# Feed-forward features transposed by DVE in 32x32 blocks and placed by DMAs through DRAM, with gate and up chunks issued ahead of the down parts

## The chip, the cores and the metric

The kernel runs on one core of one Trainium2 chip. What is measured is the device time of one execution, in microseconds (us), lower is better. The engines are named as in the profile: PE (TensorE matmul), PEld (its weight load), DVE (VectorE), ACT (ScalarE), POOL (GpSimd) and SP (SyncE, which here only issues DMAs; "SPq" is its queue).

## The reference

A stack of four transformer layers and then one hybrid block, for 256 tokens of width 1024, all in float32. The mixers of the four layers are differential attention, stick-breaking attention, sliding-window attention with sinks, and differential attention again. The part that the change touches is the feed-forward block that ends each of the four layers:

```python
D_MODEL = 1024; SEQ = 256; DEPTH = 4
FFN_HIDDEN = -(-8 * D_MODEL // (3 * 256)) * 256        # 2816

def swiglu(h, w_gate, w_up, w_down):
    return (jax.nn.silu(h @ w_gate) * (h @ w_up)) @ w_down

for i in range(DEPTH):
    hn = rms_norm(x, norm_gains[i, 0])
    ...                                                # m = the mixer of layer i
    x = x + rms_norm(m, norm_gains[i, 1])
    f = swiglu(rms_norm(x, norm_gains[i, 2]), ffn_w_gate[i], ffn_w_up[i], ffn_w_down[i])
    x = x + rms_norm(f, norm_gains[i, 3])
```

## The kernel before

**Tiles.** The 256 tokens are two blocks b = 0 and 1 of 128 tokens. All big products keep float32 accuracy by splitting each operand into a high part that the matmul takes exactly (`hi`) and the rest (`lo`), and adding three matmuls: hi x hi, hi x lo, lo x hi. The stationary operand is the transposed activations (features on the 128 partitions, tokens along the row): `hnT` for the normalised input of a layer, `hT` for the hidden features of the feed-forward block, `oT` for the output of a mixer. The moving operand is a 128x512 piece of a weight matrix. A `gemm` over a contraction of 1024 is thus 8 x 3 = 24 matmuls into one PSUM tile `acc`.

**Weights.** All weights are streamed. A chunk is 512 columns of a weight matrix. SP loads it in `raw` tiles (three buffers of 1 MB); for each half of a `raw` tile ACT writes `hi` and DVE writes `lo` into a `w` tile (11 buffers, four of them to a chunk). A `w` tile is free again when both blocks have used it.

**Steps.** The work is a list of steps, one for each chunk, and block 1 runs one step behind block 0: (step 1, b 0), (step 0, b 1), (step 2, b 0), and so on. In the feed-forward block a gate step makes silu(gate) into `sg`, an up step multiplies it in (`scalar_tensor_tensor` on DVE), and the product, 128 tokens x 512 features, must become four 128x128 columns of `hT`. Before, `xpose_split` does this: four PE transposes into the PSUM tile `tr`, then `hi` by ACT and `lo` by DVE into `hT`. The 2816 hidden features are five groups of 512 (gate and up as chunks of their own) and a last group of 256 (`gate_up`, one chunk with both). They are contracted in three parts of 8, 8 and 6 columns (groups 0 and 1, groups 2 and 3, groups 4 and 5), each with two down chunks (j = 0, 1) whose sums are collected in `facc`. The tile `hT` has one buffer for each block, so the `hT` of a part can only be written when the part before has been used up.

**Order of the instructions.** Nothing is issued in the order of the code. Each operation is recorded, with its dependencies, the order in which buffers of a ring are reused, and an estimated cost; `schedule` then tries many list schedules with randomly drawn priorities (`seed`), keeps the one whose estimate is shortest, and `issue` writes it out as a fixed order for each engine. Every engine works through its own list strictly in order, and waits at an instruction whose inputs are not ready. All instructions are issued from one line of the file, so the profile's rows all read L522 and are told apart by the names of the tiles.

Of the kernel before, what the change touches and what calls it, by code (L numbers as in the profile page):

```python
# [10 lines left out]
F32 = mybir.dt.float32  # L11
# [3 lines left out]
AF = mybir.ActivationFunctionType  # L15
ALU = mybir.AluOpType
# [4 lines left out]
P = 128  # L21
D = 1024
KT = D // P
# [93 lines left out]
class _Program:  # L117
# [14 lines left out]
    DRAIN = 110.0  # L132
    SPARE = 3000.0
    window = 6
    tries, local, seed = 60, 120, 3
    pace = 1.1
    stick, stick_back = 3000.0, 1e9

# [390 lines left out]
class _Net:  # L529
# [711 lines left out]
    def ffn_steps(self, li):  # L1241
        nc, a = self.nc, self.a
        wg, wu, wd = a["ffn_w_gate"][li], a["ffn_w_up"][li], a["ffn_w_down"][li]
        st = {}

        def begin(b):
            if b == 0:
                st["g_post"] = self.load_gain(a["norm_gains"][li, 3])
                st["facc"] = self.S8("facc").rearrange("p (b n) -> p b n", b=NB)
            st["hnT", b], st["r", b] = self.prenorm(b, 2 * li + 1)  # L1250

        def gate_up(ch, part, kt):
            def fn(b):
                ps = self.gemm(b, st["hnT", b], ch)
                s, n = self.t2g(b, "sg"), ch.n // 2
                nc.scalar.activation(s[:, :n], ps[:, :n], AF.Silu, scale=st["r", b])
                nc.vector.scalar_tensor_tensor(s[:, :n], ps[:, n:], st["r", b], s[:, :n], op0=ALU.mult, op1=ALU.mult)
                self.xpose_split(b, s, st["hT", part, b], kt, n=n // P)
            return fn

        def gate(ch, first):
            def fn(b):
                if first:
                    begin(b)
                ps = self.gemm(b, st["hnT", b], ch)
                s = self.t2g(b, "sg")
                nc.scalar.activation(s[:, :ch.n], ps[:, :ch.n], AF.Silu, scale=st["r", b])
                st["sg", b] = s
            return fn

        def up(ch, part, kt):
            def fn(b):
                ps = self.gemm(b, st["hnT", b], ch)
                s = st["sg", b]
                nc.vector.scalar_tensor_tensor(s[:, :ch.n], ps[:, :ch.n], st["r", b], s[:, :ch.n], op0=ALU.mult,
                                               op1=ALU.mult)
                if kt == 0:
                    st["hT", part, b] = self.TB(b, "hT")
                self.xpose_split(b, s, st["hT", part, b], kt, n=ch.n // P)
            return fn  # L1280

        def down(ch, part, j):
            def fn(b):
                ps = self.gemm(b, st["hT", part, b], ch)
                f = st["facc"][:, b, j * 512:(j + 1) * 512]
                if part == 0:
                    nc.scalar.activation(f, ps, AF.Copy)
                else:
                    nc.vector.tensor_tensor(f, ps, f, op=ALU.add)
                if part == 2 and j == 1:  # L1290
                    self.postnorm(b, [st["facc"][:, b, 0:512], st["facc"][:, b, 512:1024]], st["g_post"])
            return fn

        base = 0
        for part, nkt in enumerate((8, 8, 6)):
            kt = 0
            while kt < nkt:
                m = min(4, nkt - kt)
                c0 = (base + kt) * P
                if m == 2:  # L1300
                    ch = self.chunk_of([(wg, c0, m * P), (wu, c0, m * P)], 0, KT)
                    self.step(ch, gate_up(ch, part, kt))
                else:
                    ch = self.chunk(wg, 0, KT, c0, m * P)
                    self.step(ch, gate(ch, part == 0 and kt == 0))
                    ch = self.chunk(wu, 0, KT, c0, m * P)
                    self.step(ch, up(ch, part, kt))
                kt += m
            for j in range(2):
                ch = self.chunk(wd, base, nkt, j * 512, 512)  # L1310
                self.step(ch, down(ch, part, j))
            base += nkt

    def ssm_prep_tasks(self):
        nc, a = self.nc, self.a
# [551 lines left out]
```

## Time and profile before

| | |
|---|---|
| median of 3 runs | 1373.03 us (1371.23 to 1373.67) |
| the profiled execution | 1374.15 us, of which the span of its instructions is 1372.3 us |
| PE busy | 1356.4 us of the span, 99% |
| DVE, ACT, POOL busy | 910.8, 769.2 and 204.9 us |
| granted TensorE clock, mean | 0.996 of full speed |
| moved by DMA | 244.72 MB, mean 178 GB/s |

The profile is of one execution. Matmuls overlap, and the busy time of a short group of matmuls contains the time in which its last one still drains; what a group costs is better read from the chain of work, which gives the distance from one group to the next. Idle time of an engine that is not the bottleneck costs nothing.

### The profile page before, as it was taken

What the parts mean: (1) busy time and instruction counts of PE and PEld (TensorE: products, weight loads), DVE (VectorE), ACT (ScalarE), POOL (GpSimd) and SP (SyncE); (2) the same over time, 40 slices, a digit from 0 to 9 for tenths busy, and PEclk for the clock granted to TensorE, in tenths of its full rate; (3) what the DMA queues carried; (4) which work ended last, traced back from release to release, by engine and by line L of the source; (5) the groups of instructions that cost most, each with busy time, mean ns of one, the idle gap of its engine ahead of it and who ended that gap; (6) DMA issues with size and microseconds to landing.
All of it is one profiled execution on the core that took longest, in us unless ns stands there. A gap on an engine that the chain in (4) does not pass through costs nothing.

```text
span 1372.3 us, 17953 instructions
## 1 busy us (share of the span) xinstructions
PE 1356.4 (99%) x6825; PEld 1119.8 (82%) x6825; DVE 910.8 (66%) x1339; ACT 769.2 (56%) x1269; POOL 204.9 (15%) x331
## 2 busy tenths in 40 slices
PE   9999999999999999999999999999999999999998
PEld 6788888888878888888778888888888888887886
DVE  7977756558665655559967545598866455686493
ACT  6667554437876544447665434465665444564582
POOL 1010067433000069202001000010000000020000
PEclk9999999999999999999999999999999999999999
DMA  8553665455442666645425555554536555476550
GB/s 305 190 185 103 238 229 190 153 204 193 153 154 92 221 220 219 196 156 167 159 87 200 184 186 182 188 170 153 184 107 245 186 184 169 148 239 189 184 192 31
DMA packets 134341, 244.72 MB, mean 178 GB/s; under 512 B 5248, under 2 KB 27008, under 8 KB 134256
## 3 DMA queue, kind: packets, MB, share of 16 engines
q1 hardware_dynamic: 134256, 243.59, 52.8%
q8 instruction: 53, 0.87, 0.3%
q14 instruction: 32, 0.26, 0.1%
HBM read 236.90 MB, written 6.67 MB: 177 GB/s over the span
## 4 chain that ended last, share of the span: by engine, by line
PE 89%; DVE 6%; DMA 2%; ACT 1%; issue 1%; POOL 0%; SPq 0%; ACTq 0%; DVEq 0%
PE acc L522 77%; PE tr L522 3%; DVE w L522 2%; PE z L522 1%; PE sS L522 1%; PE sc L522 1%; DVE rp L522 1%; DMA raw<-in_a_w_in_dram 1%; PE o L522 1%; DVE q L522 1%; PE Y L522 1%; PE asT L522 1%; PE oB L522 0%; PE oC L522 0%; DMA raw<-in_w_ple_gate_dram 0%
## 5 line engine op out<-in xcount | busy, mean ns | idle before, releaser
L522 PE MATMUL acc<-w,hnT 128*128 128x512 f32 (+1 forms) x3552 | 842.8, 391 | 2.1 <-ACT w L522 1.3
L522 PEld LDWEIGHTS acc<-w,hnT 128*128 128x128 f32 x3552 | 651.9, 189 | 135.3 <-ACT w L522 2.1
L522 DVE TENSOR_TENSOR w<-raw,w 128x1024 fp32r<-128x1024 f32 (+1 forms) x431 | 518.6, 1219 | 180.6 <-ACT w L522 170.5
L522 ACT ACTIVATE w<-raw 128x1024 fp32r<-128x1024 f32 (+1 forms) x431 | 442.0, 1041 | 184.4 <-PE acc L522 149.4
L522 PE MATMUL acc<-w,hT 128*128 128x512 f32 x1056 | 252.8, 392 | 0.4 <-DVE hT L522 0.4
L522 PEld LDWEIGHTS acc<-w,hT 128*128 128x128 f32 x1056 | 196.0, 188 | 40.4 <-DVE hT L522 0.8
L522 PE MATMUL acc<-w,oT 128*128 128x512 f32 x480 | 119.9, 397 | 0.0
L522 PEld LDWEIGHTS acc<-w,oT 128*128 128x128 f32 x480 | 88.7, 188 | 18.1 <-issue 0.3
L522 POOL TENSOR_TENSOR po_r<-po_v,neghalf 128x1 f32<-128x1 f32 x16 | 11.9, 746 | 478.4 <-DVE po_v L522 478.4
L522 ACT ACTIVATE sg<-acc,pn_r 128x512 f32<-128x512 f32 (+1 forms) x48 | 31.0, 649 | 86.8 <-PE acc L522 86.8
L522 DVE SCALAR_TENSOR_TENSOR sg<-acc,pn_r,sg 128x512 f32<-128x512 f32 (+1 forms) x48 | 33.8, 705 | 58.9 <-PE acc L522 35.0
L522 POOL TENSOR_TENSOR pg<-pg 128x128 f32<-128x128 f32 x96 | 61.6, 669 | 38.5 <-DMA pg<-scrP 36.0
L522 ACT ACTIVATE hT<-tr 128x512 fp32r<-128x512 f32 (+1 forms) x48 | 26.6, 556 | 53.3 <-PE tr L522 53.2
L522 DVE TENSOR_TENSOR hT<-tr,hT 128x512 fp32r<-128x512 f32 (+1 forms) x48 | 30.7, 642 | 27.0 <-ACT hT L522 27.0
L522 POOL TENSOR_TENSOR pn_r<-pn_v,neghalf 128x1 f32<-128x1 f32 x20 | 17.6, 882 | 189.9 <-DVE pn_v L522 175.1
L522 DVE TENSOR_TENSOR facc<-acc,facc 128x512 f32<-128x512 f32 x32 | 21.9, 686 | 33.0 <-PE acc L522 32.9
L522 ACT ACTIVATE hnT<-gx 128x512 fp32r<-128x512 f32 x36 | 22.7, 630 | 26.5 <-DVE gx L522 26.4
L522 POOL TENSOR_TENSOR pt<-pp 128x256 f32<-128x256 f32 x32 | 28.9, 914 | 42.3 <-PE ke L522 41.6
L522 ACT ACTIVATE ad_e<-sc,ad_nm 128x128 f32<-128x128 f32 (+1 forms) x64 | 26.1, 421 | 12.9 <-DVE ad_nm L522 12.5
L522 ACT ACTIVATE sqj<-x 128x512 f32<-128x512 f32 x40 | 24.9, 623 | 11.3 <-DVE x L522 10.8
L522 POOL TENSOR_TENSOR ad_r<-ad_v,neghalf 128x4 f32<-128x4 f32 x8 | 9.5, 1182 | 135.4 <-DVE ad_v L522 135.4
L522 DVE TENSOR_TENSOR hnT<-gx,hnT 128x512 fp32r<-128x512 f32 x36 | 25.3, 704 | 4.8 <-ACT hnT L522 4.2
(232 smaller groups left out, 1119.4 us busy)
## 6 DMA issues: line engine op xcount, KB each, us to landing
raw<-in_ffn_w_gate_dram SPq DMA_DIRECT2D x40, 1024.0 KB, 5.2
raw<-in_ffn_w_up_dram SPq DMA_DIRECT2D x40, 1024.0 KB, 5.1
raw<-in_ffn_w_down_dram SPq DMA_DIRECT2D x32, 1024.0 KB, 5.2
raw<-in_a_w_in_dram SPq DMA_DIRECT2D x22, 1024.0 KB, 5.2
raw<-in_ffn_w_down_dram SPq DMA_DIRECT2D x16, 768.0 KB, 4.6
raw<-in_b_w_in_dram SPq DMA_DIRECT2D x12, 1024.0 KB, 5.2
raw<-in_w_in_dram SPq DMA_DIRECT2D x12, 1024.0 KB, 5.2
raw<-in_a_w_out_dram SPq DMA_DIRECT2D x8, 1024.0 KB, 5.0
```

The costliest lines, as they stand in the source:

```text
L522: r = getattr(getattr(self.nc, op.eng), op.call)(*op.args, **op.kw)
```

## The change

For the five groups of 512 features, the up step no longer transposes on PE. DVE transposes the product in 32x32 blocks (one instruction, `transpose`, into a tile `hx`), four DMAs of 64 KB put the rows of 32 partitions each in their place in a scratch tensor in DRAM (`scrH`), and one DMA of 256 KB loads it back as `hl`, now with features on the partitions. ACT writes `hi` and DVE `lo` of `hT` from `hl`. `hx` and `hl` come from the ring `t2a`, three tiles of 128x512 for each block. The last group of 256 still goes through PE.

The steps get another order. Before: groups 0, 1, down part 0, groups 2, 3, down part 1, groups 4, 5, down part 2. After: groups 0, 1, 2, down part 0, groups 3, 4, down part 1, group 5, down part 2. So a part's down steps follow the gate and up of one more group. The features of groups 2 and 4 have no place in `hT` until the down steps of the part before are done, so their `load` is recorded behind these. The seed of the schedule search changes from 3 to 6, and as the search runs over the whole program, the order of the instructions changes everywhere.

```diff
@@ -132,7 +132,7 @@
-    tries, local, seed = 60, 120, 3
+    tries, local, seed = 60, 120, 6
@@ -1268,16 +1268,35 @@
-        def up(ch, part, kt):
+        def up(ch, g, now):
             def fn(b):
                 ps = self.gemm(b, st["hnT", b], ch)
                 s = st["sg", b]
                 nc.vector.scalar_tensor_tensor(s[:, :ch.n], ps[:, :ch.n], st["r", b], s[:, :ch.n], op0=ALU.mult,
                                                op1=ALU.mult)
-                if kt == 0:
-                    st["hT", part, b] = self.TB(b, "hT")
-                self.xpose_split(b, s, st["hT", part, b], kt, n=ch.n // P)
+                t = self.t2a(b, "hx")
+                nc.vector.transpose(t.rearrange("p (q c t) -> p c q t", q=4, c=4),
+                                    s.rearrange("p (c q h) -> p c q h", c=4, q=4))
+                d = self.dp.tile([4, P, P], F32, name=f"scrH{li}_{g}_{b}")
+                for i in range(4):
+                    nc.sync.dma_start(out=d[i].rearrange("(q h) x -> h q x", q=4),
+                                      in_=t[32 * i:32 * i + 32].rearrange("h (q x) -> h q x", q=4))
+                st["d", g, b] = d
+                if now:
+                    load(g, b)
             return fn
+
+        def load(g, b):
+
+            part, kt = g // 2, 4 * (g % 2)
+            if kt == 0:
+                st["hT", part, b] = self.TB(b, "hT")
+            t = self.t2a(b, "hl")
+            nc.sync.dma_start(out=t.rearrange("p (i x) -> p i x", i=4), in_=st["d", g, b].rearrange("i p x -> p i x"))
+            v = t.rearrange("p (i c t) -> p c i t", i=4, c=4)
+            hi, lo = (st["hT", part, b][:, kt:kt + 4, i, :].rearrange("p c (i t) -> p c i t", i=4) for i in range(2))
+            nc.scalar.activation(hi, v, AF.Copy)
+            nc.vector.tensor_tensor(lo, v, hi.bitcast(F32), op=ALU.subtract)
 
         def down(ch, part, j):
             def fn(b):
@@ -1287,29 +1306,26 @@
                     nc.scalar.activation(f, ps, AF.Copy)
                 else:
                     nc.vector.tensor_tensor(f, ps, f, op=ALU.add)
+                if part < 2 and j == 1:
+                    load(2 * part + 2, b)
...
-        base = 0
-        for part, nkt in enumerate((8, 8, 6)):
...
+        for g, part in ((0, None), (1, None), (2, 0), (3, None), (4, 1), (5, 2)):
+            c0 = g * 512
+            if g < 5:
+                ch = self.chunk(wg, 0, KT, c0, 512)
+                self.step(ch, gate(ch, g == 0))
+                ch = self.chunk(wu, 0, KT, c0, 512)
+                self.step(ch, up(ch, g, g not in (2, 4)))
+            else:
+                ch = self.chunk_of([(wg, c0, 256), (wu, c0, 256)], 0, KT)
+                self.step(ch, gate_up(ch, 2, 4))
+            if part is not None:
+                for j in range(2):
+                    ch = self.chunk(wd, 8 * part, 6 if part == 2 else 8, j * 512, 512)
+                    self.step(ch, down(ch, part, j))
```

On PE, at the beginning of the feed-forward block of the fourth layer, these rows stood before (`acc<-w,hnT` are the matmuls of gate and up, `acc<-w,hT` those of down, `tr<-ident,sg` the transposes of the features):

```order
L522 MATMUL acc<-w,hnT 128x512 x81
L522 MATMUL tr<-ident,sg 128x128 x4
L522 MATMUL acc<-w,hnT 128x512 x24
L522 MATMUL tr<-ident,sg 128x128 x4
L522 MATMUL acc<-w,hT 128x512 x24
L522 MATMUL acc<-w,hnT 128x512 x24
L522 MATMUL acc<-w,hT 128x512 x24
L522 MATMUL tr<-ident,sg 128x128 x4
L522 MATMUL acc<-w,hT 128x512 x24
```

The same place on PE now:

```order
L522 MATMUL acc<-w,hnT 128x512 x7
L522 MATMUL tr<-ident,x_108 128x128 x4
L522 MATMUL acc<-w,hnT 128x512 x209
L522 MATMUL acc<-w,hT 128x512 x22
L522 MATMUL acc<-w,hnT 128x512 x2
L522 MATMUL acc<-w,hT 128x512 x6
L522 MATMUL acc<-w,hnT 128x512 x21
```

The transposes of `sg` are gone, and a longer run of gate and up matmuls (209) stands ahead of the first down matmuls.

On SP, at the same place, the queue held only weights and one row of gains before:

```order
L522 DMA raw<-in_ffn_w_gate_dram 128x4x512 x2
L522 DMA raw<-in_ffn_w_up_dram 128x4x512
L522 DMA g<-in_norm_gains_dram 128x1024
L522 DMA raw<-in_ffn_w_up_dram 128x4x512
L522 DMA raw<-in_ffn_w_down_dram 128x4x512 x4
```

The same place on SP now (the names of the scratch tensors are scrH, the group, the block and a number):

```order
L522 DMA scrH_0_0_1698<-hx 32x4x128 x4
L522 DMA hl<-scrH_0_0_1698 128x4x128
L522 DMA raw<-in_ffn_w_gate_dram 128x4x512 x2
L522 DMA raw<-in_ffn_w_up_dram 128x4x512 x2
L522 DMA scrH_0_1_1723<-hx 32x4x128 x4
L522 DMA scrH_1_0_1734<-hx 32x4x128 x4
L522 DMA raw<-in_ffn_w_down_dram 128x4x512
L522 DMA hl<-scrH_0_1_1723 128x4x128
L522 DMA hl<-scrH_1_0_1734 128x4x128
L522 DMA raw<-in_ffn_w_down_dram 128x4x512 x3
L522 DMA scrH_1_1_1748<-hx 32x4x128 x4
```

Here the weight loads of the next group stand in SP's list behind the four writes and the load of a group's features, each of which waits for the one ahead of it to finish.

## Rows read from the trace of the kernel before

**Rows 1.** The page, busy time of each engine: us (share of the span) xinstructions.
```profile
PE 1356.4 (99%) x6825; PEld 1119.8 (82%) x6825; DVE 910.8 (66%) x1339; ACT 769.2 (56%) x1269; POOL 204.9 (15%) x331
```
**Rows 2.** Windows by stage: stretch, length, busy per engine, PEclk, DMA share, GB/s.
```profile
12.00:127.00 115.00, 112.63 (x563) 92.70 (x563) 96.59 (x178) 76.49 (x181) 9.14 (x12) 0.99 0.56 194
127.00:310.00 183.00, 183.00 (x870) 152.61 (x869) 112.88 (x142) 90.86 (x115) 80.07 (x155) 1.00 0.58 198
310.00:440.00 130.00, 129.49 (x678) 105.85 (x678) 87.80 (x117) 96.03 (x153) 13.21 (x15) 1.00 0.45 152
440.00:608.00 168.00, 167.99 (x764) 138.72 (x762) 97.03 (x96) 82.90 (x98) 62.69 (x98) 1.00 0.60 199
608.00:731.00 123.00, 120.92 (x737) 100.73 (x735) 98.15 (x205) 77.11 (x185) 10.66 (x15) 1.00 0.44 144
731.00:895.00 164.00, 164.00 (x746) 135.74 (x745) 90.84 (x97) 77.96 (x95) 3.18 (x6) 1.00 0.55 187
895.00:1033.00 138.00, 137.13 (x695) 114.40 (x694) 113.45 (x183) 86.02 (x197) 9.67 (x10) 1.00 0.49 164
1033.00:1201.00 168.00, 168.00 (x768) 139.08 (x767) 95.20 (x100) 82.29 (x101) 2.26 (x5) 1.00 0.55 182
1201.00:1345.00 144.00, 141.17 (x896) 116.98 (x895) 106.61 (x198) 88.93 (x130) 13.65 (x11) 0.98 0.58 191
```
**Rows 3.** The chain that ended last, 140 to 260 us: start, us, what.
```profile
167.08 0.44 PE tr L522 x4
167.52 16.38 PE acc L522 x72
183.90 0.44 PE tr L522 x4
184.33 27.23 PE acc L522 x120
211.56 0.44 PE tr L522 x4
```
**Rows 4.** Instructions that touch the tile tr: ns min/median/max, first and last start.
```profile
L522 PE MATMUL tr<-ident,sg x176: 270/272/308, 142.0 to 1198.3; 128*128 128x128 f32 x176
```
**Rows 5.** Groups on DVE and ACT, shapes apart: busy us, mean ns | idle before.
```profile
L522 DVE TENSOR_TENSOR w<-raw,w 128x1024 fp32r<-128x1024 f32 x413 | 507.0, 1243 | 175.2 <-ACT w L522 165.2
L522 DVE SCALAR_TENSOR_TENSOR sg<-acc,pn_r,sg 128x512 f32<-128x512 f32 x40 | 30.0, 749 | 44.8 <-PE acc L522 35.0 <-ACT sg L522 9.6
L522 DVE TENSOR_TENSOR hT<-tr,hT 128x512 fp32r<-128x512 f32 x40 | 27.4, 687 | 26.8 <-ACT hT L522 26.8
L522 DVE COPY pt<-pp 64x64 f32<-64x64 f32 x16 | 6.2, 387 | 0.2
L522 ACT ACTIVATE hT<-tr 128x512 fp32r<-128x512 f32 x40 | 23.6, 592 | 51.4 <-PE tr L522 51.3
L522 ACT ACTIVATE hnT<-gx 128x512 fp32r<-128x512 f32 x36 | 22.7, 630 | 26.5 <-DVE gx L522 26.4
```
**Rows 6.** Tile scrG: its DMA issues on SP, in ns, and its landing times.
```profile
L522 SPq DMA_DIRECT2D scrG<-pg x32: 508/596/954, 500.5 to 557.4; - x32
...
DMA to landing us min/median/max: 2.0/3.1/9.0
```
**Rows 7.** DMA issues: xcount, KB each, median us to landing.
```profile
raw<-in_ffn_w_gate_dram SPq DMA_DIRECT2D x40, 1024.0 KB, 5.2
...
scrE<-scrE SPq DMA_DIRECT2D x4, 512.0 KB, 5.1
scrG<-scrG SPq DMA_DIRECT2D x2, 1024.0 KB, 7.8
```
**Rows 8.** Waits of the SP queue: us in total, times, longest us.
```profile
SPq L522 <- DVE w L522: 976.5, 184, 19.1
```
**Rows 9.** Timeline of the third layer's feed-forward, SP, ACT and PE apart.
```profile
754.67 3.11 SPq L522 DMA_DIRECT2D raw<-in_ffn_w_gate_dram  x2
...
763.69 1.06 ACT L522 ACTIVATE w<-raw 128x1024 fp32r<-128x1024 f32 x1 [0.76 <-PE acc L522]
...
778.94 5.60 PE L522 MATMUL acc<-w,hnT 128*128 128x512 f32 x24
```

More of the change, by code (lines that the diff above doesn't have):

```diff
@@ L1292, in down @@
             return fn
-        base = 0
-        for part, nkt in enumerate((8, 8, 6)):
[L1296 to L1312, printed above, removed]
+        for g, part in ((0, None), (1, None), (2, 0), (3, None), (4, 1), (5, 2)):
[12 more added lines that the diff above has]
+                    self.step(ch, down(ch, part, j))
     def ssm_prep_tasks(self):
```

## The prediction

> **What bounds the kernel now.** I read the page's busy times first: PE is busy for 1356.4 us, 99% of the span, and no other engine comes near it [rows 1]. A busy PE need not be a PE at its best, so the second view is the table of windows by stage [rows 2]. The four feed-forward blocks are about the stretches 127 to 310, 440 to 608, 731 to 895 and 1033 to 1201 us. In them PE is busy for 183.00 of 183.00, 167.99 of 168.00, 164.00 of 164.00 and 168.00 of 168.00 us, with the clock granted in full (1.00): it waits for nothing. DVE is busy there for 55 to 62% of the time (90.84 of 164 to 112.88 of 183 us), ACT for less. So in these stretches an instruction taken off PE shortens the program by what it held PE for, as long as the weights and the features still come in time. In the mixers between them PE's idle time is small as well: over the nine windows from 12 to 1345 us it sums to 2.37 + 0 + 0.51 + 0.01 + 2.08 + 0 + 0.87 + 0 + 2.83 = 8.7 us.
>
> The third view is the chain, which gives the pitch. A run of 120 feed-forward matmuls lasts 27.23 us [rows 3], so one takes 0.227 us and a gemm of 24 of them 5.45 us. Four transposes of `sg` between two runs take 0.44 us. The mean duration of one transpose, 272 ns [rows 4], is not its price, because they overlap.
>
> **What is removed.** There are 176 transposes of `sg` [rows 4]: 40 sets of four for the groups of 512 (4 layers x 5 groups x 2 blocks) and 8 sets of two for the last groups, which stay. 40 x 0.44 us = **17.6 us** leave PE. The ACT and DVE instructions that read `tr` (592 and 687 ns) are replaced by the same two reading `hl`. The nearest ACT row with an SBUF source is 630 ns [rows 5], which is 40 x 0.04 = 1.5 us over the whole program on an engine that is half idle: nothing on the path.
>
> **What DVE gets.** 40 block transposes of 128x512. The trace of before has none. The lower bound is the two-operand row of that size, 687 ns; the upper one the slowest copy in the trace, 64x64 in 387 ns, which is 6.0 ns per element of a row, or 3.1 us for 512 [rows 5]. I take 0.7 us, as both operands are whole rows of 512 like in the first. One group of gate and up takes PE 4 x 5.45 = 21.8 us; in that time DVE has 8 x 1.243 for the weights, 2 x 0.749 and 2 x 0.687, together 12.8 us [rows 5], and the transposes make it 14.2 us, or 19.0 us at the upper bound. Both fit in 21.8, so the term is nothing on the path. The Trainium skill, page "VectorE: DVE Perf Modes", section "The three transpose paths", gives 311 ns for a 128x128 bf16 transpose on VectorE, in 32x32 blocks; four of these would be an estimate of 1.24 us here, and DVE's sum 15.3 us, which alters nothing in the total either.
>
> **What the queue and the DMA engines get.** Each set adds four writes of 64 KB and one load of 256 KB, 200 DMAs in all. The nearest writes are those of `scrG`, also 64 KB in 128 pieces of 512 bytes: 0.596 us to issue (at most 0.954), 3.1 us to land (2.0 to 9.0) [rows 6]. The nearest loads from scratch land in 5.1 us for 512 KB and 7.8 us for 1024 KB [rows 7]; I take 5.1. The way of one set is then 0.75 (the product) + 0.7 + 4 x 0.6 + 3.1 + 0.6 + 5.1 + 0.63 + 0.69 = **14.0 us**, where PE transposes needed 0.44 + 0.59 + 0.69. At the upper bounds (3.1, 0.954, 9.0 and 7.8) it is 0.75 + 3.1 + 5 x 0.954 + 9.0 + 7.8 + 0.63 + 0.69 = 26.7 us. What hides it is the new order of steps: between the end of up of group 1 (or 3) and the first down matmul of its part, block 0 has five gemms of its own and of block 1 ahead of it, 5 x 5.45 = 27.2 us; the 209 matmuls in a row on PE show them. Group 4 has seven. Its `hT` is free only when down part 1 has ended, and from there three gemms, 16.4 us, cover the load, ACT and DVE (5.1 + 0.63 + 0.69). Without that cover each set would cost PE 14.0 us. So the term is nothing, with little room left at the upper bounds.
>
> The weight loads now stand behind these DMAs on SP. Issued in 0.6 us each, 8 writes, 2 loads and 4 weight loads take 8.4 us of a group's 21.8, and two waits for landing 6.2: 14.6 us. A wait there is covered by the lead of the weights. The loads of one gate chunk were issued at 754.67 us and land about 5.2 later, but ACT could split them only at 763.69, waiting for PE to release a `w` tile, and PE used them first at 778.94 [rows 7, 9]: 24.3 us from issue to use, about 15 from the split. SP itself spends 976.5 us waiting for buffers [rows 8]. Nor are the DMA engines full. They are busy for 0.55 to 0.60 of the feed-forward stretches at 182 to 199 GB/s [rows 2]. A layer adds 10 x 512 KB = 5.2 MB to about 33 MB (168 us x 199 GB/s), 16%; at the efficiency of the weights the share becomes 0.70, and at that of the 7.8 us row against 5.2 it is 0.74. And before there was already a like burden: 32 writes of `scrG` from 500.5 to 557.4 us, one in 1.8 us between weight loads [rows 6], where the change has 8 in 21.8 us, and PE lost nothing in that stretch [rows 2].
>
> **What is planned anew.** The search draws another seed over another program, so every mixer is reordered. From the trace, its worth is bounded by PE's idle time between 12 and 1345 us, 8.7 us: a better plan gains at most that, and a worse one I let lose as much. I take 0.
>
> **The sum.** 1374.15 us (the profiled execution) - 17.6 = 1356.5 us; the median of the runs shown is 1.1 us below that execution, which gives 1355.4. I predict 1356 us, and 1347 to 1366 for this case alone.
>
> **The rivals.** *Features come late* (part of the gain is lost). A load of `hl` stands behind weight loads that wait for a buffer, 976.5 / 184 = 5.3 us on average and 19.1 at the longest [rows 8]. With the mean a set takes 14.0 + 5.3 = 19.3 us and stays covered; with the longest it takes 33.1, and PE stands for 33.1 - 27.2 = 5.9 us. There are eight places of this kind (parts 0 and 1 in four layers). If two of them are hit, 11.8 us are given back: 1368 us. Against it: the feed-forward waits are short where weights are far ahead.
>
> *No change*: DVE takes over as the bound in the feed-forward blocks. It needs a block transpose of (22.7 - 12.8) / 2 = 4.9 us (22.7 is a group's time with its PE transposes), above the upper bound of 3.1. Time 1374 us.
>
> *Slower*: SP becomes the bound. If each set's writes hold the queue for the longest landing, 9.0 us [rows 6], a group needs 8.4 + 18.0 = 26.4 us on SP against 21.8 on PE, 4.6 us too much, and 20 groups cost 92 us: 1448 us. It decides from a landing of (21.8 - 8.4) / 2 = 6.7 us, and eats the whole gain at 7.1. For it: each load is issued only after its four writes have landed, often at the next place in the list. Against it: the median of 3.1 and the stretch of 500 to 557 us. The Trainium skill, page "VectorE: DVE Perf Modes", section "Rules for kernel authors", speaks on this side: it says to transpose 128x128 on TensorE where a PSUM destination will do. By that rule the time would go up; the trace so far supports it only in the latency of a set, not in what binds.
>
> **How the numbers follow.** 0.76 for the forecast, 0.10 for features that come late, 0.05 for no change, 0.09 for the queue. Faster by over 0.2% (about what a measurement of this kernel can tell from no change) is 0.86, within it 0.05, slower 0.09. The range of 1347 to 1370 us takes in the first two cases with the bounds of the new plan, and leaves out the last two and a little of the first.
>
> **What the profile after would show.** Right: no `tr<-ident,sg` but 16 in sets of two; PE still busy for all of the feed-forward stretches, each about 4.4 us shorter; block transposes near 0.7 us; landings of `scrH` near 3 us and of `hl` near 5; no wait of PE for `hT`. Wrong: waits of PE for `hT` or `w` in these stretches, weight loads that SP issues less than about 10 us ahead of use, or mixers that are longer by more than 9 us together.

## The result, and the profile after

The changed kernel takes 1349.49 us (median of 4 runs, 1348.86 to 1349.69) against 1372.67 us before (4 runs); the ratio is 0.9826 with a 95% interval of 0.9814 to 0.9838. It is 23.2 us faster, inside the range of 1347 to 1370 us and 6.5 us under the predicted 1356. The profiled execution took 1349.69 us, its span is 1347.9 us.

The page's busy times, which answer to [rows 1]:

```profile
PE 1333.6 (99%) x6665; PEld 1101.8 (82%) x6665; DVE 937.2 (70%) x1379; ACT 763.9 (57%) x1266; POOL 212.8 (16%) x331
```

PE has 160 instructions less and is busy for 22.8 us less, and is still the bound. The windows by stage answer to [rows 2]; the stretches are cut by hand for this run, so their lengths do not compare one by one with those before, and the columns are length, PE, PEld, DVE, ACT, POOL, clock, DMA share and GB/s:

```profile
12.00:118.00 106.00, 104.97 (x535) 86.47 (x534) 93.48 (x173) 73.95 (x177) 8.30 (x11) 1.00 0.58 199
118.00:300.00 182.00, 182.00 (x842) 151.29 (x841) 121.97 (x154) 93.24 (x116) 84.18 (x150) 1.00 0.71 234
...
424.00:594.00 170.00, 170.00 (x767) 140.56 (x766) 107.38 (x112) 85.71 (x103) 64.36 (x98) 1.00 0.73 236
...
702.00:872.00 170.00, 170.00 (x757) 140.53 (x755) 104.76 (x113) 85.64 (x106) 3.07 (x6) 1.00 0.67 219
...
1003.00:1178.00 175.00, 174.77 (x780) 144.29 (x779) 110.55 (x121) 90.73 (x115) 3.26 (x6) 1.00 0.66 216
1178.00:1320.00 142.00, 138.72 (x897) 115.42 (x895) 107.61 (x199) 85.17 (x128) 12.17 (x11) 1.00 0.60 197
```

In the feed-forward stretches PE still waits for next to nothing (0.23 us of the last one). The granted clock is 1.00 in the first and the last row as well, where [rows 2] had 0.99 and 0.98; the section on seeds comes back to this. DVE rose from 55 to 62% to 62 to 67%, the DMA engines from 0.55 to 0.60 to 0.66 to 0.73. The chain of work in the third layer shows what PE does there now, where [rows 3] had a set of transposes after runs of 72 and 120 matmuls:

```profile
716.05 0.44 PE tr L522 x4
716.49 143.53 PE acc L522 x633
```

That is 633 matmuls in 143.53 us, 0.227 us each, without a break up to the end of the window that was read. The groups on DVE and ACT, shapes apart, answer to [rows 5] (busy us, mean ns, idle before):

```profile
L522 DVE STREAM_TRANSPOSE hx<-sg 128x512 f32<-128x512 f32 x40 | 28.3, 707 | 0.8
L522 DVE TENSOR_TENSOR hT<-hl,hT 128x512 fp32r<-128x512 f32 x40 | 28.1, 701 | 37.8 <-ACT hT L522 37.7
...
L522 ACT ACTIVATE hT<-hl 128x512 fp32r<-128x512 f32 x40 | 25.0, 625 | 30.9 <-DMA hl<-scrH 25.2 <-PE acc L522 5.7
```

The DMA issues by size, median us to landing, and the instructions on the tile `scrH` (ns min/median/max) answer to [rows 6, 7]:

```profile
scrH<-hx SPq DMA_DIRECT2D x160, 64.0 KB, 2.7
hl<-scrH SPq DMA_DIRECT2D x40, 256.0 KB, 5.0
```
```profile
L522 SPq DMA_DIRECT2D scrH<-hx x160: 302/432/1556, 137.0 to 1144.2; - x160
L522 SPq DMA_DIRECT2D hl<-scrH x40: 359/377/620, 142.4 to 1147.8; - x40
```

The four writes of a group do not wait for one another; in the third layer SP issues the first four in 1.79 us, where one takes 2.7 us to land (timeline of SP):

```profile
715.63 1.79 SPq L522 DMA_DIRECT2D scrH<-hx  x4
```

Only the load behind them waits, for all four. The description of the change, by which each DMA waits for the one ahead of it, is too strict.

The waits of the SP queue, us in total, times and longest, answer to [rows 8]:

```profile
SPq L522 <- DVE w L522: 744.7, 173, 23.1
SPq L522 <- DVE hx L522: 89.4, 37, 7.6
...
SPq L522 <- DMA scrH<-hx: 16.0, 17, 4.5
```

SP waits 89.4 us for the block transposes and, at 17 of the 40 loads, 16.0 us for writes to land, and still has 744.7 us in which it waits for a free buffer. And the timeline of the third layer, SP, ACT and PE apart, for the gate chunk of group 3, answers to [rows 9]:

```profile
762.21 2.65 SPq L522 DMA_DIRECT2D raw<-in_ffn_w_gate_dram  x2
...
770.28 1.06 ACT L522 ACTIVATE w<-raw 128x1024 fp32r<-128x1024 f32 x1 [0.76 <-PE acc L522]
...
783.91 0.39 PE L522 MATMUL acc<-w,hnT 128*128 128x512 f32 x1
```

The loads are issued 21.7 us ahead of their first use (24.3 before), and split 13.6 us ahead of it. The split still begins when PE releases a `w` tile, not when the load has landed.

### The profile page after: what moved, and what is told of

Read it like the earlier page. It is cut to its first block, busy times and chain, and to the rows that moved or that the text cites. A ratio compares the mean times of both kernels' runs of the same rounds, so it can differ in the third digit from the quotient of the medians.

```text
span 1347.9 us, 17977 instructions
## 1 busy us (share of the span) xinstructions
PE 1333.6 (99%) x6665; PEld 1101.8 (82%) x6665; DVE 937.2 (70%) x1379; ACT 763.9 (57%) x1266; POOL 212.8 (16%) x331
## 4 chain that ended last, share of the span: by engine, by line
PE 82%; DVE 10%; ACT 3%; issue 2%; DMA 2%; POOL 1%; SPq 0%; ACTq 0%; POOLq 0%; DVEq 0%
PE acc L522 74%; DVE w L522 4%; PE tr L522 2%; PE z L522 1%; ACT w L522 1%; PE sc L522 1%; DVE rp L522 1%; PE sS L522 1%; DMA raw<-in_w_ple_gate_dram 1%; PE o L522 1%; DVE scA L522 1%; DMA raw<-in_w_in_dram 1%; ACT as_e L522 1%; PE oB L522 0%; DVE q L522 0%
## 5 line engine op out<-in xcount | busy, mean ns | idle before, releaser
L522 PE MATMUL acc<-w,hnT 128*128 128x512 f32 (+1 forms) x3552 | 831.1, 389 | 1.7 <-DVE w L522 1.0
L522 DVE TENSOR_TENSOR hT<-hl,hT 128x512 fp32r<-128x512 f32 x40 | 28.1, 701 | 37.8 <-ACT hT L522 37.7
L522 POOL TENSOR_TENSOR pn_r<-pn_v,neghalf 128x1 f32<-128x1 f32 x20 | 14.8, 738 | 177.9 <-DVE pn_v L522 177.3
L522 ACT ACTIVATE hT<-hl 128x512 fp32r<-128x512 f32 x40 | 25.0, 625 | 30.9 <-DMA hl<-scrH 25.2
L522 POOL TENSOR_TENSOR pp<-pp 128x16 f32<-128x16 f32 x57 | 24.3, 454 | 66.7 <-DMA pp<-in_ssm_dram 59.6
```

What stands on the lines that cost most here:

```text
L522: r = getattr(getattr(self.nc, op.eng), op.call)(*op.args, **op.kw)
```

## The experiments

All ratios are to the kernel before, run on the same chip beside it. "In its own order" means that the search made the changed kernel's plan, and only the writing-out of it was altered, so that PE, DVE, ACT and SP have the changed kernel's order with the extra instructions put in.

### The PE transposes put back into the same plan

```diff
+                nc.ops[-1].label = lambda: self.xpose_now(b, s)      # behind the block transpose
...
                 r = getattr(getattr(self.nc, op.eng), op.call)(*op.args, **op.kw)
+                if op.label is not None:
+                    op.label()
...
+    def xpose_now(self, b, src):
+        ps = self.trp.tile([P, 4, P], F32, tag=f"tr{b}", name="trx")
+        for j in range(4):
+            self.tc.nc.tensor.transpose(ps[:, j, :], src[:, j * P:(j + 1) * P], self.ident)
```

Expected: 

> The changed kernel in its own order of instructions, with the 40 sets of four PE transposes issued again behind the block transposes; their result is not used. Theory (PE is the bound, and a set is worth its pitch of 0.44 us wherever it stands): 1349.5 + 17.6 = 1367 us, 1365 to 1369. Rival (most of the 23 us come from the new plan, and a set fits into PE's idle time): under 1360 us.

Measured: 1370.1 us (9 runs), ratio 0.9978 (0.9968 to 0.9987), against 0.9826 for the changed kernel: 1.52% of 1373 us, or 20.9 us for 40 sets. The rival is out. The chain in the first layer shows the price of a set, the rows of the tile `trx` the waits for `sg`, and the page's busy times what came on top:

```profile
139.79 15.67 PE acc L522 x69
155.46 0.44 PE trx L793 x4
155.90 5.04 PE acc L522 x22
160.94 0.44 PE trx L793 x4
161.38 18.62 PE acc L522 x82
```
```profile
L793 PE MATMUL trx<-ident,sg x160: 269/272/329, 137.6 to 1164.3; 128*128 128x128 f32 x160
its engine sat idle before it (us, times) until:
  DVE sg L522: 2.2, 3
```
```profile
PE 1352.4 (99%) x6825; PEld 1116.9 (82%) x6825; DVE 938.0 (69%) x1379; ACT 763.5 (56%) x1266; POOL 211.2 (15%) x331
```

A set costs 0.44 us as before, 17.6 us together. Between the two profiled executions (spans of 1368.5 and 1347.9 us) PE's busy time rises by 18.8 us and its idle time by 1.8. The 2.2 us of waits for `sg` are those of PE and of its weight loads added up; PE itself waits for `sg` once, for 0.7 us, since these transposes stand right behind the product and not where a search would put them. The remaining 1 to 2 us were not followed further.

### Order of steps, and seeds

The order alone: PE transposes as before, the new order of steps, seed 6.

```diff
-                t = self.t2a(b, "hx")
...
-                st["d", g, b] = d
+                st["s", g, b] = s
                 if now:
                     load(g, b)
...
-            nc.scalar.activation(hi, v, AF.Copy)
-            nc.vector.tensor_tensor(lo, v, hi.bitcast(F32), op=ALU.subtract)
+            self.xpose_split(b, st["s", g, b], st["hT", part, b], kt)
```

Expected: 

> PE transposes as before, but the new order of steps and seed 6; the features of groups 2 and 4 are transposed behind the down steps. Theory (the order by itself gives nothing, the rest beyond 17.6 us is the luck of a plan): 1367 to 1373 us, 17.6 us or more above the changed kernel. Rival (the freer order of steps makes the gain): 1350 to 1360 us.

The kernel before with seed 6 (`tries, local, seed = 60, 120, 6`), expected: 

> The kernel before with seed 6 instead of 3, nothing else. Theory (the 5.6 us beyond the transposes belong to the plan that is drawn): within 9 us of 1372.7, and if the seed itself is the luck, 1367. Rival (the removal of the transposes makes the plans better): 1372 to 1380 us.

The changed kernel with seed 3 (`tries, local, seed = 60, 120, 3`), expected: 

> The changed kernel with seed 3 instead of 6, nothing else. Theory: 1355 us (1372.7 less 17.6), 1347 to 1364, so a loss against seed 6 of about 5 us. Rival (the removal of the transposes makes the plans better, whatever the seed): 1347 to 1352 us.

When these had shown that the seed is worth some 5 us on either kernel, four more were run, with seeds 1 and 2. Before with seed 1, expected: 

> The kernel before with seed 1. Theory (a plan is worth some us either way, and the transposes 17.6 to 18.9 us under any seed): 1367 to 1380 us. Rival (seed 6 is better than seed 3 by chance of only two draws of another cause, and plans do not differ): 1372 to 1375 us.

Changed with seed 1, expected: 

> The changed kernel with seed 1. Theory: the time of the kernel before with seed 1 less 18 us, give or take 5 for the two plans; 1349 to 1362 us. Rival (the removal of the transposes makes the plans better, or worse, by itself): a difference to the kernel before with seed 1 that lies under 12 or over 24 us.

Before with seed 2, expected: 

> The kernel before with seed 2. Theory: 1367 to 1380 us, as with seed 1. Rival: 1372 to 1375 us.

Changed with seed 2, expected: 

> The changed kernel with seed 2. Theory: the time of the kernel before with seed 2 less 18 us, give or take 5; 1349 to 1362 us. Rival: a difference to the kernel before with seed 2 that lies under 12 or over 24 us.

| seed | before: us, ratio | changed: us, ratio | difference of the ratios, in us of 1373 |
|---|---|---|---|
| 3 | 1372.67, 1 | 1355.17, 0.9865 | 18.5 |
| 6 | 1368.44, 0.9964 | 1349.49, 0.9826 | 18.9 |
| 1 | 1373.22, 1.0000 | 1358.04, 0.9892 | 14.8 |
| 2 | 1372.51, 1.0000 | 1358.14, 0.9893 | 14.7 |
| order alone, 6 | 1370.71, 0.9980 | | |

The intervals of the single ratios are 0.0009 to 0.0019 to either side. Under one seed the change is worth 14.7 to 18.9 us, 16.7 on average over these four; the theory's 17.6 lies among them, and the rival of a gain that comes from better plans as such (over 24 us, or 1347 to 1352 us for the changed kernel with seed 3) is out. By the ratios, seed 6 takes 5 us off the kernel before and 5 to 9 us off the changed one, against the other three. Seeds 1, 2 and 3 of the kernel before lie within 1 us of each other; its runs with seeds 1 and 2 lie in the theory's range and in the rival's narrower one, and so do not decide between the two. The order alone, with PE transposes and seed 6, is 2 us behind the kernel before with that seed (0.9980 against 0.9964): in this one draw it gives nothing by itself.

What makes the plan of seed 6 better is known only in part. In the changed kernel with seed 2, whose profiled span is 1358.0 us, PE is busy for

```profile
PE 1339.9 (99%) x6665; PEld 1101.5 (81%) x6665; DVE 938.6 (69%) x1379; ACT 761.4 (56%) x1266; POOL 216.3 (16%) x331
```

so of the 10.1 us between the two spans 6.3 are busy time of the same number of PE instructions and 3.8 are idle time. Part of the busy time is the granted clock. In the hybrid block at the end PE waits for a load of `scrE`, another scratch tensor. PE's timeline there, for the kernel before, the changed kernel with seed 2 and the changed kernel with seed 6:

```profile
1247.70 2.62 PE L522 MATMUL S<-ssm,scrE 128*64 128x31 f32 x48 [2.30 <-DMA scrE<-scrE]
...
1237.55 1.92 PE L522 MATMUL S<-ssm,scrE 128*64 128x31 f32 x32 [1.74 <-DMA scrE<-scrE]
...
1229.86 1.12 PE L522 MATMUL S<-ssm,scrE 128*64 128x31 f32 x32 [1.39 <-DMA scrE<-scrE]
```

And the windows of 6 us behind these waits, in the same order (the clock is the third number from the end):

```profile
1248.00:1254.00 6.00, 6.00 (x68) 4.95 (x65) 1.42 (x3) 2.93 (x5) 1.16 (x1) 0.50 0.86 297
...
1238.00:1244.00 6.00, 6.00 (x39) 5.01 (x38) 3.75 (x8) 3.33 (x5) 0.00 (x0) 0.50 0.92 309
...
1230.00:1236.00 6.00, 6.00 (x57) 5.15 (x56) 1.43 (x2) 2.52 (x4) 0.00 (x0) 1.00 1.00 355
```

Before and with seed 2 the clock stood at 0.50, the lower of its two levels (1.2 GHz), in these 6 us; with seed 6 it stayed at the upper one (2.4 GHz). At 0.50, 6 us hold the work of 3, so at least 3.0 of the 6.3 us are clock, an estimate from these rows.

The first stretch of the kernel before has a shorter drop of the same kind (0.50 from 13 to 15 us, behind waits of 1.33 and 0.53 us for weights). With both, [rows 2] against the windows after gives about 115 x 0.01 + 144 x 0.02 = 4.0 us of clock, and 17.6 + 4.0 is most of the 22.8 us by which PE's busy time fell. All this is of the profiled executions.

The clock changes from run to run, and it is not the whole of the seed: with a mean granted clock of 1.000 the kernel before took 1371.1 to 1371.6 us (four runs), and the changed kernel with seed 2 1356.8 to 1359.3 us (three runs), still 7 us or more above seed 6. Nothing was run that tells which pieces of the order make the rest.

### More load on the queue, and on DVE

Each of the 160 writes issued a second time, in its own order, to a tensor that nobody reads:

```diff
+                    nc.ops[-1].label = self.again(z[i], t, i)            # behind each write
...
+    def again(self, z, t, i):
+        return lambda: self.tc.nc.sync.dma_start(
+            out=z.rearrange("(q h) x -> h q x", q=4), in_=t[32 * i:32 * i + 32].rearrange("h (q x) -> h q x", q=4))
```

Expected: 

> The changed kernel in its own order, with each of the 160 writes of features issued a second time, to a scratch tensor that nobody reads. Theory (the queue has room: a group's DMAs take about 8 of its 21.8 us): 1349.5 us, at most 2 us more, and weight loads still far ahead of their use. Rival (SP is near its bound): over 1354 us, with waits of PE for w or hT in the feed-forward stretches.

Measured: 1353.88 us (1351.27 to 1355.26), ratio 0.9856 (0.9842 to 0.9869). This is 4 us more than the changed kernel, above the 2 us that I allowed and just below the rival's bound. Who waits for `scrH` and `hl`, and the waits of PE:

```profile
  ACT hT L522: 68.9, 21
```
```profile
PE acc L522 <- ACT w L522: 1.8, 2, 1.1
PE acc L522 <- DVE w L522: 1.6, 3, 0.8
PE acc L522 <- DVE sg L522: 1.5, 1, 1.5
```

In the changed kernel PE's waits for weights are

```profile
PE acc L522 <- DVE w L522: 1.0, 2, 0.8
...
PE acc L522 <- ACT w L522: 0.6, 1, 0.6
```

ACT waits 68.9 us for loads from scratch (25.2 in the changed kernel), but no wait of PE for `hT` appears, and only about 2 us more for weights. Of the 3.8 us between the two profiled spans, about 1.7 are not the queue's: the granted clock was 0.57 from 12 to 16 us, long before the first write at 138.8 us, and 1.00 there in the changed kernel. The queue has room for twice the writes; whether wholly for nothing cannot be told from four runs that spread over 4 us.

Each block transpose issued four times in a row, in its own order:

```diff
+                nc.ops[-1].label = 4                                      # on the block transpose
...
-                r = getattr(getattr(self.nc, op.eng), op.call)(*op.args, **op.kw)
+                for _ in range(op.label or 1):
+                    r = getattr(getattr(self.nc, op.eng), op.call)(*op.args, **op.kw)
```

Expected: 

> The changed kernel in its own order, with each block transpose issued four times in a row; 120 x 0.711 = 85 us more on DVE. Theory (a group leaves DVE 21.8 - 14.2 us, of which this takes 4.3): 1349.5 us, at most 4 us more. Rival (DVE is near its bound in the feed-forward blocks): over 1357 us.

Measured: 1362.66 us, ratio 0.9923 (0.9910 to 0.9937): 13 us more, where the theory allowed 4. The time is the rival's (over 1357 us). PE's waits, us in total, times, longest:

```profile
PE acc L524 <- DVE hnT L524: 4.5, 4, 1.6
PE acc L524 <- DVE w L524: 4.2, 5, 1.8
PE acc L524 <- ACT w L524: 1.5, 1, 1.5
```

Four of these waits, one in each feed-forward block (1.6, 1.0, 1.0 and 0.9 us in the windows of the four stretches), are for `hnT`, the input of the block. The timeline of the first one, DVE and PE apart, shows the place:

```profile
137.62 2.94 DVE L524 STREAM_TRANSPOSE hx<-sg 128x512 f32<-128x512 f32 x4
140.48 0.65 DVE L524 TENSOR_TENSOR hnT<-gx,hnT 128x512 fp32r<-128x512 f32 x1
...
141.18 9.15 PE L524 MATMUL acc<-w,hnT 128*128 128x512 f32 x39 [1.57 <-DVE hnT L524]
```

In DVE's fixed list the subtraction that finishes half of `hnT` stands behind the block transpose of the first group. So a group's room of 7.6 us, worked out for the steady run, is not there at the entry, where DVE still has the input of block 1 to finish. Of the 12.3 us between the two profiled spans, 4.5 are these waits, 4.1 are waits for weights beyond the 1.6 of the changed kernel, and 2.2 are longer busy time of PE; the rest was not traced further. For the change itself this means that one transpose of 0.71 us fits, and that a slow one (3.1 us, the upper bound, is 4.4 of them) would, by this run and in this order, have cost over 10 us.

### The detour without the new order, and the order without the detour's DMAs

The detour alone, seed 6, with the down steps at once behind their groups:

```diff
-                if part < 2 and j == 1:
-                    load(2 * part + 2, b)
...
-        for g, part in ((0, None), (1, None), (2, 0), (3, None), (4, 1), (5, 2)):
+        for g, part in ((0, None), (1, 0), (2, None), (3, 1), (4, None), (5, 2)):
...
-                self.step(ch, up(ch, g, g not in (2, 4)))
+                self.step(ch, up(ch, g, True))
```

Expected: 

> Block transposes and DMAs as in the changed kernel, seed 6, but the old order of steps, so that the down steps follow their own groups at once. Theory (only the new order hides the way through DRAM, 12.6 us by the changed kernel's rows against a cover of one gemm and twelve matmuls, 8.2 us): PE waits 4.4 us at eight places, 1385 us, at least 1360. Rival (the planner finds cover without it): 1343 to 1356 us.

Measured: 1358.17 us, ratio 0.9895 (0.9879 to 0.9911), between the theory's lower bound and the rival's range. The theory falls: the way through DRAM is hidden without the new order as well, up to a difference of 9 us to the changed kernel. The changed kernel with seeds 1 and 2 takes as much; whether the 9 us belong to the order of steps or to the plan drawn was not tested with another seed. The timeline of the third layer, DVE, ACT and PE apart, shows how:

```profile
735.07 0.71 DVE L522 STREAM_TRANSPOSE hx<-sg 128x512 f32<-128x512 f32 x1
...
750.78 0.61 ACT L522 ACTIVATE hT<-hl 128x512 fp32r<-128x512 f32 x1
...
720.33 33.37 PE L522 MATMUL acc<-w,hnT 128*128 128x512 f32 x144
753.54 12.40 PE L522 MATMUL acc<-w,hT 128*128 128x512 f32 x54
```

A run of 144 gate and up matmuls, six gemms, stands before the first down matmul. The second group of that down step is transposed by DVE at 735.07 us, with 18.5 us of the run still to come, and ACT writes it into `hT` at 750.78. So the search put work of block 1 ahead of the down step of block 0, and made the cover that I had counted as missing (8.2 us). The rows of the tile `hl`, under who waited for it, show that little is left uncovered:

```profile
  PEld acc L522: 3.2, 5
  PE acc L522: 1.1, 2
```

These are the waits of PE and of its weight loads for such features in the whole run.

Without DRAM: DVE and ACT read the block-transposed tile itself.

```diff
-                d = self.dp.tile([4, P, P], F32, name=f"scrH{li}_{g}_{b}")
...
-                st["d", g, b] = d
+                st["d", g, b] = t
...
-            t = self.t2a(b, "hl")
-            nc.sync.dma_start(out=t.rearrange("p (i x) -> p i x", i=4), in_=st["d", g, b].rearrange("i p x -> p i x"))
+            t = st["d", g, b]
```

Expected: 

> The changed kernel without its DMAs: ACT and DVE read the block-transposed tile itself, so the blocks are not put in their places and the features are wrong. Order of steps and seed 6 as in the change, planned anew. Theory (the way through DRAM is wholly hidden): 1349.5 us, give or take 6 for another plan. Rival (the DMAs cost something, in queue or DMA engines): under 1343 us.

Measured: 1355.88 us, ratio 0.9871 (0.9857 to 0.9884), 6 us more than the changed kernel although it does less, and just outside the theory's range. It was planned anew, and a seed draws another plan for another program; plans differ by as much, so this run speaks against the rival, that the DMAs cost 6 us or more, and does not show that they cost nothing.

## Why the prediction was right, point by point

- **PE as the bound of the feed-forward blocks**: right. PE is busy for 182.00 of 182.00, 170.00 of 170.00 twice, and 174.77 of 175.00 us after the change. That each stretch gets 4.4 us shorter cannot be read from stretches that were cut by hand twice; the last down matmuls of the four layers end 8.5, 13.8, 19.0 and 21.9 us earlier than before.
- **17.6 us for 40 sets of 0.44 us**: right. Put back into the same plan they cost 20.9 us, of which 17.6 are the sets at their pitch; under equal seeds the change is worth 16.7 us on average.
- **DVE's block transpose, 0.7 us**: 0.707. The Trainium skill's figure for a 128x128 bf16 tile, 311 ns in "VectorE: DVE Perf Modes", section "The three transpose paths", taken four times, made an estimate of 1.24 us; the measurement decides, and a 128x512 float32 tile takes 0.707 us. That it costs nothing is right for this size, but the room which I read from the steady run is not there at the entry of a block.
- **The way through DRAM, 14.0 us, hidden**: it is 0.75 + 0.71 + 4 x 0.43 + 2.7 + 0.38 + 5.0 + 0.63 + 0.70 = 12.6 us by the rows after, and PE never waits for `hT`. The longest landing of a write was 7.3 us, within the bound of 9.0; the longest issue, 1.56 us, was above the bound of 0.954 without harm.
- **What hides it**: only half right. The new order of steps gives cover, but the step "without that cover each set would cost PE 14.0 us" failed: without the new order the search finds other cover, PE and its weight loads wait 4.3 us in all for such features, and the detour alone takes 1358 us.
- **The lead of the weights**: right, 21.7 us in place of 24.3. The DMA engines' share of 0.70 to 0.74 became 0.66 to 0.73.
- **The new plan, taken as 0 within 8.7 us**: the seed gave 5 to 9 us. This is the whole distance from 1356 to 1349.5: with seeds 3, 1 and 2 the changed kernel takes 1355.17, 1358.04 and 1358.14 us, so the 6.5 us beyond the forecast are the luck of seed 6. The bound drawn from PE's idle time held by luck as well, as its reason failed: between seeds 6 and 2 PE's busy time differs by 6.3 us, for the same number of instructions, and its idle time by only 3.8. The term that was left out stood in [rows 2]: a granted clock of 0.99 and 0.98 in the first and the last stretch, about 4 us that are busy time and no idle time.
- **The rival of features that come late**: did not happen; ACT waits 25.2 us for `hl` in nine places, and PE for none of it. **The queue as the bound**: did not happen; SP keeps 744.7 us of waiting for buffers. Waits for landings, which the prediction put at 6.2 us a group, 124 us in 20 groups, came to 16.0 us. The Trainium skill's advice to transpose on TensorE, "VectorE: DVE Perf Modes", section "Rules for kernel authors", did not hold here: where PE never waits, four transposes of 0.44 us on PE cost more than 12.6 us of latency elsewhere.

## What to carry to other kernels

On the engine that is busy without a gap, price an instruction by the distance that it puts between its neighbours on the chain, not by its duration (four transposes: 0.44 us, against 272 ns each), and move it to any engine or queue with room, even by a way that is seven times as long, as long as enough other work lies between producer and consumer. Read room for the new work at the entry of a stage too, not only in its steady run. And where a search orders the program, run both versions under several seeds before the difference is put down to the change: here a seed alone was worth 5 to 9 us, and the change 15 to 19. Read the granted clock along with the busy time, since a slower clock looks like busy time.

## What the runs showed of the hardware

The block transpose on DVE took 0.697 to 0.712 us for a 128x512 float32 tile, hardly more than a two-operand subtraction of that size (0.687 us before, 0.701 after), although it reads and writes through strided views. A write of 64 KB in pieces of 512 bytes to DRAM landed in 2.7 us (1.6 to 7.3) and the load of 256 KB in 5.0 us (2.6 to 8.1), beside a stream of weights; together they kept the DMA engines busy for up to 73% of a feed-forward stretch. Behind a wait of 2.30 us of PE the granted clock was 0.50 for at least 6 us, and with it the same matmuls took longer as busy time.
